# Start of a hybrid encoder block: input norm to first queries in a written order, norm weights as one row spread by TensorE, splits on VectorE, five PSUM banks for the first gates

## The chip, the cores and the metric

The kernel runs on one core of a Trainium2 chip. A core has TensorE (PE, matrix products; its weight loads are shown apart as PEld), VectorE (DVE), ScalarE (ACT) and GpSimd (POOL), which work side by side and wait for each other through semaphores; each takes its own instructions strictly in the order in which the program lists them. SyncE (SP) here only issues transfers. Operands lie in SBUF, the products of PE in PSUM banks of 128 x 512 fp32. The metric is the device time of one execution in microseconds, the median of three runs. A difference under about 0.2% can't be told from none.

## The reference

One layer of a bidirectional encoder over 1024 tokens of width 1024 with 16 learned meta tokens in front. All of it is fp32. The start, which is what this case is about, is

```python
a = rms_norm(h, norm_mix[l])                  # h: 16 meta rows, then x
(q_na, k_na, v_na, q_hg, z_f, z_b, i_hg, g_hg, gate_na, gate_hg) = split_cols(a @ w_in[l])
qh = silu(heads(q_hg))                        # 4 heads of 128
log_f = logaddexp(log(lb), log1p(-lb) + log_sigmoid(z))   # per direction
k = -expm1(log_f)
o = chunk_scan(qh, k_f, v, lf_f) + rev(chunk_scan(rev(qh), rev(k_b), rev(v), rev(lf_b)))
```

`rms_norm` multiplies each row by the inverse root of its mean square and by the weights `norm_mix`. Behind the recurrence (HGRN2) come a neighbourhood attention, two gated output projections, a product with `w_o`, an MLP with squared ReLU, and a last norm.

## The kernel before

**Products.** Every product with the input norm's result `a` is made of three: both operands are split into a high part (`hi`, rounded) and the rest (`lo`), and PE adds hi·hi, hi·lo and lo·hi in one PSUM bank (`mm3`, L134). `a` is kept transposed in `aT`: two halves of 512 tokens, each with a high and a low part of 8 x 128 rows; the 16 meta tokens are 16 more columns of half 0.

**The norm** (`norm_transpose`, L99) works on blocks of 128 rows: ACT squares the block with a running sum (`na`, L105), POOL makes the inverse root from it (`rtm`, `rs`, L92 and L93), DVE multiplies block, root and weights in one instruction (L107), PE transposes the result in two times four pieces (`pt`, L111), ACT rounds each four to the high part (L114), and DVE subtracts it to get the low part (L115). The weights `g_bc` are needed on all 128 partitions: one transfer reads the row 128 times (L155). The order is the meta block first, then blocks 0 to 7.

**The weight blocks.** `load_block` (L118) brings 1024 x 128 of `w_in` into `raw`, ACT makes `hi`, and another engine `lo`. There are two buffers of each. For the first two blocks, ZF and ZB (the forward and backward gates of head 0), `lo` is made by POOL, for all others by DVE.

**The gates of head 0** (`gates_of`, L250). ZF is three products: tokens 0 to 255, 256 to 511 with the 16 meta columns (272 columns), and 512 to 1023. ZB is two of 512. Two sigmoids on ACT (`sf`, `sn`) and three operations on DVE (into `T`, `X`, `Y`) evict each. The first three products are taken in the order ZF, ZF, ZB, then the second halves.

**Head 0's chain** (`hgrn`, L290). DVE multiplies neighbouring elements of `T` level by level (`TN`, L302). Queries: 48 products of block Q, two of 512 tokens; ACT a sigmoid, DVE `q` (L316) and `QQ` (L318). POOL adds X and Y to `kd` (L370); then PE makes the scores of `kd` and `q` (L374). For each level PE makes scores of `X` and `QQ` (L390), DVE makes the next `X` (a COPY of Y, L396, and a product, L397), and POOL the next `Y` (L399).

**The order of the work.** Each engine's list is set by the tile scheduler from the program text: an instruction may be placed earlier than it is written. Transfers are issued by SP in the order of the text. PSUM is eight banks: two `mm` and one `mx` for the products' turn, three `a` for transposes and scores, two `b`:

```python
psum_pools(mx=1, a=3, b=2)
```

Of the kernel before, what the change touches and what calls it, by code (L numbers as in the profile page):

```python
# [9 lines left out]
F32 = mybir.dt.float32  # L10
# [8 lines left out]
P = 128  # L19
# [29 lines left out]
def layer(ctx: ExitStack, tc: tile.TileContext, x, meta, w_in, w_na, w_hg, w_o, w_up, w_dn,  # L49
# [27 lines left out]
    psum_pools(mx=1, a=3, b=2)  # L77
# [21 lines left out]
    def norm_transpose(sp_pool, src, g_bc, dst, c0, n, nbuf):  # L99

        ssq = sp_pool.tile([P, 1], F32, tag="ssq", name="ssq", bufs=4)
        rs = sp_pool.tile([P, 1], F32, tag="rs", name="rs", bufs=4)
        tm = sp_pool.tile([P, 1], F32, tag="rtm", name="rtm", bufs=4)
        a = sp_pool.tile([P, D], F32, tag="na", name="na", bufs=nbuf)
        act.activation(a[:n], src, AF.Square, accum_out=ssq[:n])  # L105
        rsqrt_mean(rs[:n], ssq[:n], D, tm[:n])
        dve.scalar_tensor_tensor(a[:n], src, rs[:n], g_bc[:n], op0=ALU.mult, op1=ALU.mult)  # L107
        for j in range(2):
            pt = bank("a", "pt")
            for k in range(4):  # L110
                pe.transpose(pt[:, k, :n], a[:n, (4 * j + k) * P:(4 * j + k + 1) * P], ident[:n, :n])  # L111
            hi = dst[0][:, 4 * j:4 * j + 4, c0:c0 + n]
            lo = dst[1][:, 4 * j:4 * j + 4, c0:c0 + n]
            act.copy(hi, pt[:, :, :n])  # L114
            dve.tensor_tensor(lo, pt[:, :, :n], hi.bitcast(F32), op=ALU.subtract)  # L115


    def load_block(src, kc, scale=None, eng=dve):  # L118

        raw = wp.tile([P, KC, P], F32, tag="raw", name="raw")  # L120
        hi = wp.tile([P, KC, P], F32R, tag="hi", name="hi")
        lo = wp.tile([P, KC, P], F32R, tag="lo", name="lo")
        sp.dma_start(raw[:, :kc], src.rearrange("(k p) c -> p k c", p=P))
        if scale is None:
            act.copy(hi[:, :kc], raw[:, :kc])  # L125
            eng.tensor_tensor(lo[:, :kc], raw[:, :kc], hi[:, :kc].bitcast(F32), op=ALU.subtract)  # L126
# [19 lines left out]
    with tc.tile_pool(name="p0", bufs=1) as p0:  # L146
        g_bc = p0.tile([P, D], F32, name="g_bc")
        xm = p0.tile([NM, D], F32, name="xm")
        xt = [p0.tile([P, D], F32, tag="xt", name="xt", bufs=8) for _ in range(8)]

        def load_x(i):
            sp.dma_start(xt[i], x[i * P:(i + 1) * P, :])
        load_x(0)
        sp.dma_start(xm, meta)
        sp.dma_start(g_bc, g_mix.rearrange("(o d) -> o d", o=1).broadcast_to([P, D]))  # L155
        load_x(1)
        load_x(2)
# [1305 lines left out]
```

## Time and profile before

| | us |
|---|---|
| median of three runs | 1539.89 (1538.74 to 1540.42) |
| the profiled execution: its run, its span | 1543.13, 1541.4 |
| PE busy, of the span | 1500.9 (97%) |
| DVE, ACT, POOL busy | 1030.8, 658.0, 386.7 |
| mean granted clock of PE | 0.997 |

The profiled execution is one more run, 3.2 us above the median of the others. Its span is the time from the first to the last instruction on the core. A line of a timeline gives start, duration, engine, line of the kernel, operation, output and inputs, and in brackets how long the engine stood idle before it and what ended that.

### The profile page before, as it was taken

The numbers are of one execution on the slowest core, as the hardware profiler recorded it, in microseconds if no ns is written. First come the engines' busy times: TensorE is split into PE (matmuls) and PEld (weight loads), VectorE is DVE, ScalarE is ACT, GpSimd is POOL, SyncE is SP. The second block draws the span as 40 slices with busy tenths as digits, with TensorE's granted clock in tenths as the row PEclk, the third lists the DMA queues.
The fourth block names the chain that finished last, engine by engine and source line by source line (L and its number), as shares of the span: only waits on it lengthen the run. The fifth ranks groups of instructions, "written<-read, shape, count | busy, mean of one in ns | idle before, by whom it ended". The sixth has DMA issues, their size and how long they took to land.

```text
span 1541.4 us, 23453 instructions
## 1 busy us (share of the span) xinstructions
PE 1500.9 (97%) x9188; PEld 1253.1 (81%) x9188; DVE 1030.8 (67%) x1601; ACT 658.0 (43%) x1173; POOL 386.7 (25%) x355
## 2 busy tenths in 40 slices
PE   5999999999999999999999999999999999999998
PEld 5788888877888887888888887888888888888886
DVE  6666666664966877666566358877777544877876
ACT  6231313124665667434224135555555533434444
POOL 4313122216225310010000122444433200232142
PEclk9999999999999999999999999999999999999999
DMA  5101011113123127434747123444444676563224
GB/s 181 43 28 56 29 56 29 56 29 117 61 72 119 50 76 253 149 119 163 247 163 240 47 79 130 158 153 152 155 151 151 204 266 236 194 233 117 96 82 151
DMA packets 142591, 196.13 MB, mean 127 GB/s; under 512 B 8064, under 2 KB 90112, under 8 KB 142480
## 3 DMA queue, kind: packets, MB, share of 16 engines
q1 hardware_dynamic: 133680, 173.13, 34.0%
q10 hardware_dynamic: 6624, 14.16, 2.4%
q0 software_dynamic: 2176, 7.34, 1.3%
q8 instruction: 72, 1.18, 0.3%
q14 instruction: 39, 0.32, 0.1%
HBM read 140.08 MB, written 54.53 MB: 126 GB/s over the span
## 4 chain that ended last, share of the span: by engine, by line
PE 87%; DVE 6%; issue 2%; ACT 2%; DMA 1%; POOL 1%; SPq 0%; POOLq 0%; ACTq 0%; DVEq 0%
PE mm L135 11%; PE mm L136 10%; PE mm L137 10%; PE mm L1185 5%; PE pa L1185 4%; PE pb L692 4%; PE pb L694 4%; PE pb L693 4%; PE pb L1185 4%; PE pc L1185 4%; PE pc L692 3%; PE pc L694 3%; PE pc L693 3%; PE pa L694 2%; PE pa L692 2%
## 5 line engine op out<-in xcount | busy, mean ns | idle before, releaser
L135 PE MATMUL mm<-aT,hi 128*128 128x512 f32 (+2 forms) x640 | 229.8, 359 | 2.7 <-DVE QX L563 1.5
L137 PE MATMUL mm<-aT,lo 128*128 128x512 f32 (+2 forms) x640 | 227.5, 356 | 0.0
L136 PE MATMUL mm<-aT,hi 128*128 128x512 f32 (+2 forms) x640 | 226.3, 354 | 0.0
L135 PEld LDWEIGHTS mm<-aT,hi 128*128 128x128 f32 x640 | 121.6, 190 | 17.2 <-issue 1.7
L137 PEld LDWEIGHTS mm<-aT,lo 128*128 128x128 f32 x640 | 121.5, 190 | 13.1
L136 PEld LDWEIGHTS mm<-aT,hi 128*128 128x128 f32 x640 | 121.6, 190 | 12.5
L97 DVE TENSOR_TENSOR dl<-ur,dh 128x1024 fp32r<-128x1024 f32 x54 | 71.0, 1316 | 87.3 <-ACT dh L96 87.1
L96 ACT CAST dh<-ur 128x1024 fp32r<-128x1024 f32 x54 | 56.9, 1054 | 166.4 <-issue 91.1
L125 ACT CAST hi<-raw 128x1024 fp32r<-128x1024 f32 x36 | 37.8, 1051 | 106.6 <-PE mm L136 75.5
L990 DVE TENSOR_TENSOR wl<-raw,wh 128x512 fp32r<-128x512 f32 x50 | 41.0, 823 | 36.5 <-ACT wh L989 36.3
L994 ACT ACTIVATE uv<-uv 128x512 f32<-128x512 f32 x48 | 30.4, 633 | 80.0 <-DVE uv L1102 48.9
L990 DVE TENSOR_TENSOR wl<-sx,wh 128x512 fp32r<-128x512 f32 x70 | 61.0, 882 | 3.4 <-ACT wh L989 3.3
L989 ACT CAST wh<-sx 128x512 fp32r<-128x512 f32 x70 | 42.2, 620 | 42.2 <-PE pc L693 23.9
L1275 POOL TENSOR_TENSOR w<-w,tt 128x512 f32<-128x512 f32 x16 | 23.4, 1460 | 132.9 <-DVE tt L1274 113.6
L399 POOL TENSOR_TENSOR Y<-X,TN 128x512 f32<-128x512 f32 x20 | 34.9, 1746 | 86.1 <-DVE X L396 86.1
L126 DVE TENSOR_TENSOR lo<-raw,hi 128x1024 fp32r<-128x1024 f32 x34 | 43.2, 1269 | 16.1 <-ACT hi L125 15.3
L618 DVE CUSTOM_DVE_ANT_0 pr<-nsc,NB 128x432 f32<-128x432 f32 (+1 forms) x64 | 35.2, 559 | 26.6 <-PE nsc L613 26.5
L692 PE MATMUL pb<-nt,wh 128*128 128x512 f32 x128 | 50.2, 392 | 0.3 <-DVE uv L1072 0.2
L135 PE MATMUL mm<-wh,mT 128*128 128x512 f32 x128 | 50.2, 392 | 0.0
L92 POOL TENSOR_SCALAR rtm<-ssq 128x1 f32<-128x1 f32 (+1 forms) x17 | 6.5, 385 | 173.8 <-ACT junk L920 159.3
L693 PE MATMUL pb<-nt,wh 128*128 128x512 f32 x128 | 49.8, 389 | 0.0
L694 PE MATMUL pb<-nt,wl 128*128 128x512 f32 x128 | 49.8, 389 | 0.0
(388 smaller groups left out, 4406.1 us busy)
## 6 DMA issues: line engine op xcount, KB each, us to landing
raw<-in_w_in SPq DMA_DIRECT2D x56, 512.0 KB, 4.0
ur<-usp SPq DMA_DIRECT2D x54, 512.0 KB, 3.4
raw<-in_w_up SPq DMA_DIRECT2D x16, 1024.0 KB, 6.1
usp<-us SPq DMA_DIRECT2D x60, 256.0 KB, 2.2
sg<-gsp SPq DMA_DIRECT2D x16, 512.0 KB, 3.7
w<-in_w_dn SPq DMA_DIRECT2D x16, 512.0 KB, 4.9
usp<-uv SPq DMA_DIRECT2D x30, 256.0 KB, 2.2
gsp<-gv ACTq DMA_DIRECT2D x24, 256.0 KB, 2.6
```

Source lines behind the costliest of these rows:

```text
L96: act.copy(hi, src)
L97: dve.tensor_tensor(lo, src, hi.bitcast(F32), op=ALU.subtract)
L126: eng.tensor_tensor(lo[:, :kc], raw[:, :kc], hi[:, :kc].bitcast(F32), op=ALU.subtract)
L135: pe.matmul(ps, lh, rh, start=first, stop=False)
L136: pe.matmul(ps, lh, rl, start=False, stop=False)
L137: pe.matmul(ps, ll, rh, start=False, stop=last)
L692: pe.matmul(ps, lhs[0][:, c], rhs[0][:, k], start=first and k == 0, stop=False, skip_group_check=True)
L693: pe.matmul(ps, lhs[0][:, c], rhs[1][:, k], start=False, stop=False, skip_group_check=True)
L694: pe.matmul(ps, lhs[1][:, c], rhs[0][:, k], start=False, stop=k == 3, skip_group_check=True)
L989: act.copy(v(hi), src)
L990: dve.tensor_tensor(v(lo), src, v(hi).bitcast(F32), op=ALU.subtract)
L1185: pe.matmul(ps, a[n == 2][:, q, j * P:(j + 1) * P], b[n == 1][:, q], start=first and n == 0, stop=last and n == 2, skip_group_check=True)
```

## The change

**Norm weights.** A transfer of one row of 1024 numbers, issued by ACT, takes the place of the transfer of 128 rows. PE multiplies a column of ones with the row in two products of 512 columns (`pg`), and ACT copies them to `g_bc`, ahead of its first square. The meta rows, the gates' bounds `lt` and the gain are issued by ACT as well.

**Splits.** `load_block` has no engine any more: `lo` is made by DVE for all blocks.

**Banks.** The start uses two `mm`, three `mx` and three `a`; the two `b` come in place of two `mx` once head 0's queries are written. So the five first gate products each have a bank of their own, and none of them needs an eviction to begin.

**Order.** Everything from the first instruction to head 0's queries stands inside `tc.manual_schedule`, where each engine's list is the order of the text. The text has a new function `start`, which lists the steps block by block: square, transpose, scale, evict, and some of the gate products between them. The gates' evictions are called after all five products.

```diff
-    psum_pools(mx=1, a=3, b=2)
+    psum_pools(mx=3, a=3)
...
-    def load_block(src, kc, scale=None, eng=dve):
+    def load_block(src, kc, scale=None, raw=None):
...
-            eng.tensor_tensor(lo[:, :kc], raw[:, :kc], hi[:, :kc].bitcast(F32), op=ALU.subtract)
+            dve.tensor_tensor(lo[:, :kc], raw[:, :kc], hi[:, :kc].bitcast(F32), op=ALU.subtract)
...
-        sp.dma_start(g_bc, g_mix.rearrange("(o d) -> o d", o=1).broadcast_to([P, D]))
...
+        act.dma_start(g_row, g_mix.rearrange("(o d) -> o d", o=1))
+        act.dma_start(xm, meta)
+        act.dma_start(lt.rearrange("p a b c -> p (a b c)"), lbl)
+        act.dma_start(gain_sb, gain)
...
+        for h in range(2):
+            pg = bank("a", "pg").rearrange("p a b -> p (a b)")
+            pe.matmul(pg, ones, g_row[:, h * TH:(h + 1) * TH], start=True, stop=True)
+            act.copy(g_bc[:, h * TH:(h + 1) * TH], pg)
...
+        square(0)
+        scale(0)
+        square(1)
+        pt = transpose(0)
+        scale(1)
+        evict(0, pt)
+        blocks[0] = load_block(None, KC, raw=raw_f)
+        square(2)
+        pt = transpose(1)
+        scale(2)
+        evict(1, pt)
+        square(3)
...
+        f0 = products(0, 0, 0, 256, 0, 0)
+        some(f0, 4)
+        square(4)
+        pt = transpose(3)
+        scale(4)
+        evict(3, pt)
+        some(f0, 4)
+        square(5)
+        pt = transpose(4)
+        blocks[1] = load_block(None, KC, raw=raw_b)
+        scale(5)
+        evict(4, pt)
+        b0 = products(1, 0, 0, TH, 0, 0)
+        some(b0, 2)
+        square(8)
+        pt = transpose(5)
+        scale(8)
+        square(6)
+        scale(6)
+        evict(5, pt)
+        some(b0, 3)
+        ptm = transpose(8)
+        evict(8, ptm)
+        pt = transpose(6)
+        square(7)
+        scale(7)
+        evict(6, pt)
+        some(b0, 3)
+        pt = transpose(7)
...
+        evict(7, pt)
...
+        for q in (products(0, 0, 256, 256, 256, NM), products(0, 1, 0, TH, TH, 0), products(1, 1, 0, TH, TH, 0)):
+            some(q, KC)
...
+        early[C_Q] = block_of(C_Q)
...
+    with tc.manual_schedule(engines={e.engine for e in (pe, act, dve, pool, sp)}):
+        start()
...
         list(ahead[0])
...
+        cur = hgrn(0, hp, lmask_get, tiles[0], ahead[1])
+        next(cur)
+    psum_pools(mx=1, a=3, b=2)
```

`some(f0, 4)` is four steps of three products each; block 8 is the meta block. Three places of the lists follow. In them L105 and L507 are squares, L114 and L528 the casts of a transposed block, L125 and L112 the `hi` of a weight block.

ACT's list in the norm, before and then of the change:

```order
L105 ACTIVATE na,ssq<-xm 16x1024
L105 ACTIVATE na,ssq<-xt 128x1024 x2
L114 CAST aT_90<-pt 128x4x16 x2
L105 ACTIVATE na,ssq<-xt 128x1024
L114 CAST aT_90<-pt 128x4x128
L125 CAST hi<-raw 128x1024
L114 CAST aT_90<-pt 128x4x128 x2
L105 ACTIVATE na,ssq<-xt 128x1024
L114 CAST aT_90<-pt 128x4x128 x3
L105 ACTIVATE na,ssq<-xt 128x1024 x2
L114 CAST aT_90<-pt 128x4x128 x2
```

```order
L498 COPY g_bc<-pg 128x512 x2
L507 ACTIVATE na,ssq<-xt 128x1024 x2
L528 CAST aT_87<-pt 128x4x128 x2
L112 CAST hi<-raw 128x1024
L507 ACTIVATE na,ssq<-xt 128x1024
L528 CAST aT_87<-pt 128x4x128 x2
L507 ACTIVATE na,ssq<-xt 128x1024
L528 CAST aT_87<-pt 128x4x128 x2
L507 ACTIVATE na,ssq<-xt 128x1024
L528 CAST aT_87<-pt 128x4x128 x2
L507 ACTIVATE na,ssq<-xt 128x1024
L112 CAST hi<-raw 128x1024
```

Now the copies of the weights stand first, and squares and pairs of casts alternate.

PE's list of the change at its beginning (L497 spreads the weights, L520 transposes, L122 to L124 are the three products of a step):

```order
L497 MATMUL pg<-g_row,ones 128x512 x2
L520 MATMUL pt<-ident,na 128x128 x24
L122 MATMUL mm<-aT_87,hi 128x256
L123 MATMUL mm<-aT_88,hi 128x256
L124 MATMUL mm<-aT_87,lo 128x256
```

The transposes of three blocks stand ahead of the first product; before it was those of the meta block and of two blocks.

DVE's list from the products of `T` to the second `q`, before and then of the change (L261 is `TN`, L355 and L356 the next `X`, L275 `q`, L277 `QQ`, L113 the `lo` of a weight block):

```order
L302 TENSOR_TENSOR TN<-TN 128x256
L396 COPY X<-Y 128x128x4
L302 TENSOR_TENSOR TN<-TN 128x128
L316 TENSOR_TENSOR q<-q,mm 128x512
L302 TENSOR_TENSOR TN<-TN 128x64
L318 TENSOR_TENSOR QQ<-T_385,q 128x2x512
L302 TENSOR_TENSOR TN<-TN 128x32
L397 TENSOR_TENSOR X<-X,TN 128x128x2x2
L302 TENSOR_TENSOR TN<-TN 128x16
L396 COPY X<-Y 128x64x8
L397 TENSOR_TENSOR X<-X,TN 128x64x2x4
L126 TENSOR_TENSOR lo<-raw,hi 128x1024
```

```order
L355 COPY X<-Y 128x128x4
L261 TENSOR_TENSOR TN<-TN 128x128
L356 TENSOR_TENSOR X<-X,TN 128x128x2x2
L261 TENSOR_TENSOR TN<-TN 128x64
L355 COPY X<-Y 128x64x8
L261 TENSOR_TENSOR TN<-TN 128x32
L356 TENSOR_TENSOR X<-X,TN 128x64x2x4
L261 TENSOR_TENSOR TN<-TN 128x16
L113 TENSOR_TENSOR lo<-raw,hi 128x1024
L275 TENSOR_TENSOR q<-q,mm 128x512
L277 TENSOR_TENSOR QQ<-T_524,q 128x2x512
L113 TENSOR_TENSOR lo<-raw,hi 128x1024
```

`q` stood behind one COPY of `Y`, now behind two, behind all the `TN` and behind a `lo`.

More of the change, by code (lines that the diff above doesn't have):

```diff
@@ L278, in gate @@
             return ev, (mev if d == 0 else None)
+        if done:
+            for d, ps, t0, n, nm in done:
+                ev, mev = gate(d)
+                if nm:
+                    mev(ps[:, n:])
+                ev(ps[:, :n], t0, n)
+            return
         zf = proj_steps(C_ZF + hd * P, *gate(0))
         zb = proj_steps(C_ZB + hd * P, *gate(1))
-        if hd == 0:
-            for z in (zf, zf, zb):
-                yield next(z)
         for z in (zf, zb):
```

151 lines of the change are left out of this document (94 added, 57 removed).

## The prediction

> **What bounds the kernel now.** I read the page first, then the busy time in stretches (a row has its start and end, its length, the busy time of PE, PEld, DVE, ACT and POOL, and PE's granted clock), then the instructions of the first 80 us.
>
> ```profile
> PE 1500.9 (97%) x9188; PEld 1253.1 (81%) x9188; DVE 1030.8 (67%) x1601; ACT 658.0 (43%) x1173; POOL 386.7 (25%) x355
> ...
> 9.00:32.10 23.10, 16.42 (x106) 15.25 (x106) 20.53 (x21) 16.15 (x30) 13.64 (x16) 1.00 0.54 194
> 32.10:61.10 29.00, 29.00 (x135) 23.87 (x135) 16.85 (x37) 10.95 (x22) 11.67 (x17) 1.00 0.20 58
> 61.10:70.00 8.90, 6.28 (x156) 5.74 (x156) 7.66 (x13) 1.73 (x3) 3.63 (x2) 0.85 0.21 61
> ```
>
> TensorE (PE) is busy 97% of the span; of its 40.5 us of idle time 18.3 lie before 70 us (the first 9.0, and the two pieces below). So whatever moves the first score products of head 0 moves the end by the same amount. The change acts in the two places where PE is short of work: the norm, where it stands idle for 6.7 of the 23.1 us from 9 to 32.1, and 61.1 to 70, where 2.62 are missing. In between it has no gap.
>
> The norm, in the timelines of DVE, ScalarE (ACT), GpSimd (POOL) and PE:
>
> ```profile
> 9.04 1.27 DVE L107 SCALAR_TENSOR_TENSOR na<-xm,rs,g_bc 16x1024 f32<-16x1024 f32 x1 [9.04 <-DMA g_bc<-in_g_mix]
> 10.24 1.27 DVE L107 SCALAR_TENSOR_TENSOR na<-xt,rs,g_bc 128x1024 f32<-128x1024 f32 x1
> ...
> 12.28 1.28 DVE L107 SCALAR_TENSOR_TENSOR na<-xt,rs,g_bc 128x1024 f32<-128x1024 f32 x1 [0.38 <-POOL rs L93]
> 14.28 3.48 DVE L107 SCALAR_TENSOR_TENSOR na<-xt,rs,g_bc 128x1024 f32<-128x1024 f32 x1 [0.71 <-ACT hi L125]
> ...
> 24.07 1.28 DVE L107 SCALAR_TENSOR_TENSOR na<-xt,rs,g_bc 128x1024 f32<-128x1024 f32 x1 [1.27 <-POOL rs L93]
> ...
> 26.47 1.27 DVE L107 SCALAR_TENSOR_TENSOR na<-xt,rs,g_bc 128x1024 f32<-128x1024 f32 x1
> ...
> 28.87 3.08 DVE L107 SCALAR_TENSOR_TENSOR na<-xt,rs,g_bc 128x1024 f32<-128x1024 f32 x1
> ...
> 35.88 1.29 DVE L115 TENSOR_TENSOR aT<-pt,aT 128x512 fp32r<-128x512 f32 x2 [0.27 <-ACT aT L114]
> ...
> 4.62 1.05 ACT L105 ACTIVATE na<-xm 16x1024 f32<-16x1024 f32 x1 [2.62 <-DMA xm<-in_meta]
> ...
> 10.18 1.06 ACT L105 ACTIVATE na<-xt 128x1024 f32<-128x1024 f32 x1 [3.37 <-DMA xt<-in_x]
> ...
> 26.35 1.08 ACT L114 CAST aT<-pt 128x512 fp32r<-128x512 f32 x2
> 27.31 1.07 ACT L125 CAST hi<-raw 128x1024 fp32r<-128x1024 f32 x1
> ...
> 14.33 2.35 POOL L126 TENSOR_TENSOR lo<-raw,hi 128x1024 fp32r<-128x1024 f32 x1
> ...
> 24.25 1.16 POOL L92 TENSOR_SCALAR rtm<-ssq 128x1 f32<-128x1 f32 x1 [0.21 <-ACT na L105]
> 26.43 0.19 POOL L92 TENSOR_SCALAR rtm<-ssq 128x1 f32<-128x1 f32 x1 [0.39 <-ACT na L105]
> ...
> 11.56 1.97 PE L111 MATMUL pt<-ident,na 128*128 128x128 f32 x8 [0.17 <-DVE na L107]
> ...
> 25.71 1.03 PE L111 MATMUL pt<-ident,na 128*128 128x128 f32 x8
> ```
>
> DVE starts at 9.04, when the 512 KB broadcast of the weights has landed, and its last eviction ends at 37.17. A block costs it 2.40 (24.07 to 26.47). Twice a scaling lasts 3.48 or 3.08 instead of 1.28; the first stands exactly beside POOL's split of 2.35.
>
> **The change part by part.** The sum is made against the profiled execution (span 1541.4, run 1543.13); the median of the runs is 3.2 us below that, and I carry the difference over to 1539.89.
>
> *Weights as one row.* The broadcast goes. The row leaves ACT's queue first; the 64 KB transfer of xm, the nearest row, is there at 4.62, and 4.0 is my estimate for 4 KB. The two products of 128x512 on PE are not in the trace: by the transposes, eight of 128 columns in 1.97 at the cold start, 512 columns are about 1.0 each; twice that if a plain fp32 product takes two passes. I take 1.35, two are 2.7, to 6.7. Two copies follow, 0.54 each (half of the 1.08 pair), the second behind its product: 7.3. Block 0's square stands behind them on ACT. From a square's start to its scaling takes 2.1 (10.18 to 12.28), so block 0 is scaled at 9.4 instead of 10.24: a gain of 0.8, between 0 and 1.7. Four small transfers are now issued by ACT, which has nothing else to do until the first product ends, and SP's queue loses four issues: block 1's x, whose square waited for it until 10.18, comes earlier and is hidden. Meta's block, which was scaled first, moves behind block 5 with the same work.
>
> *Splits from POOL to DVE.* DVE takes two more operations, 1.14 each (the period from 64.82 to 65.95, quoted below), and gets back 2.2 and 1.8 of the two stretched scalings: a net gain of 1.7. POOL's small operations are no longer queued behind 2.35. The Trainium skill ("SBUF — State Buffer", Who interferes with whom) says that a DVE operation with two SBUF inputs and a POOL operation that reads SBUF exclude each other for a whole instruction. The trace agrees (14.28 lasts until POOL's split is done). The rule also speaks against the change: the splits on DVE have two such inputs, and POOL's small operations will wait behind them, as the 1.16 against 0.19 shows; by it each of the 2.1 us steps below that meets a split or a scaling takes 1.0 more, and the norm's +2.6 becomes +3.6 to +4.6; by the unstretched rows it stays.
>
> *The written order of the norm.* DVE's busy time in the norm was 37.17 - 9.04 less its idle time, 28.1 - 2.8 (0.38, 0.71, 1.27, 0.27 and 0.16 of an unquoted wait) = 25.3; now 25.3 - 4.0 + 2.3 = 23.6. Without gaps it would end at 9.4 + 23.6 = 33.0. But each square now stands on ACT behind the casts of the block two before it, where before it ran up to two blocks ahead. The loop of two blocks is scaling 1.2, eight transposes 1.03 (1.97 at the slow clock), casts 1.08, square to scaling 2.1: 5.4 warm and 6.35 slow, against 4.8 of DVE's own work. Step by step: block 0 scaled at 9.4; block 2 behind a slow loop and the split's 1.05 on ACT, 16.8; block 4 one slow loop later, 23.2. Block 3's transposes stand behind 12 products of 256 columns on PE, which ran at half clock (0.21 from start to start) in the first 3 us:
>
> ```profile
> 22.11 0.41 PE L137 MATMUL mm<-aT,lo 128*128 128x256 f32 x1
> 22.32 0.41 PE L135 MATMUL mm<-aT,hi 128*128 128x256 f32 x1
> ...
> 29.35 0.29 PE L136 MATMUL mm<-aT,hi 128*128 128x272 f32 x1
> 29.47 0.29 PE L137 MATMUL mm<-aT,lo 128*128 128x272 f32 x1
> ...
> 49.83 0.39 PE L137 MATMUL mm<-aT,lo 128*128 128x512 f32 x1
> 50.06 0.39 PE L135 MATMUL mm<-aT,hi 128*128 128x512 f32 x1
> ```
>
> Twelve take 2.5. Block 2's transposes end at 16.8 + 3.2 = 20.0, block 3's at about 24.0, its casts at 25.1, and block 5's square follows. The second block's hi ends at 27.3, its lo holds DVE to 28.5, and block 5 is scaled then. The casts of block 4 end at 28.4; the squares of meta and block 6 behind them give scalings at 30.5 and 31.7. PE meanwhile: 6 products (1.4), block 5's transposes to 31.0, 9 products (2.05) to 33.1, meta's transposes to 34.1, its casts (0.5), block 7's square, and block 7 is scaled at 36.7. Its transposes end at 38.8. Behind them stand 24 products of 272 columns at 0.125 and 48 of 512 at 0.23: 3.0 + 10.9. Head 0's last gate product ends at 52.7 instead of 50.06: **+2.6**. Bounds: DVE without a gap brings the last transposes to 31.2 (33.0 less 1.8: the last two evictions, 1.29, and half a pair of casts) and the product to 45.1, -5.0; slow transposes throughout and POOL's small operations stretched each time add some 3: +5.5. I take the value of the steps, since every one is a row.
>
> *Five banks.* With them the 272 and 512 products need no eviction before they start. Evictions were no bound before (PE is busy for all of the 29 us from 32.1 to 61.1), so this removes nothing.
>
> *Gates to first queries.* On ACT the split of Q's block now stands ahead of all sigmoids, and it waits for the buffer that the last ZF product frees, 5.5 before ZB's end. Priced as casts (1.08 a pair) the six sigmoids of the first half, four of the second and the split take some 5 to 6, so they just fit under ZB's last product and I cost them at nothing; without that cover it would be up to 1.
>
> On DVE q stands behind the second COPY X<-Y and behind the split of the next block, not in front of them.
>
> ```profile
> 53.24 1.22 DVE L302 TENSOR_TENSOR TN<-T 128x1024 f32<-128x1024 f32 x1
> ...
> 56.36 0.43 DVE L302 TENSOR_TENSOR TN<-TN 128x256 f32<-128x256 f32 x1
> 59.92 0.43 DVE L396 COPY X<-Y 128x512 f32<-128x512 f32 x1 [3.13 <-POOL Y L399]
> ...
> 60.47 0.68 DVE L316 TENSOR_TENSOR q<-q,mm 128x512 f32<-128x512 f32 x1
> ...
> 64.82 1.21 DVE L126 TENSOR_TENSOR lo<-raw,hi 128x1024 fp32r<-128x1024 f32 x1
> 65.95 0.67 DVE L316 TENSOR_TENSOR q<-q,mm 128x512 f32<-128x512 f32 x1
> ...
> 53.41 4.53 POOL L370 TENSOR_TENSOR kd<-X,Y 128x512 f32<-128x512 f32 x1 [10.69 <-DVE X L270]
> 58.02 1.87 POOL L399 TENSOR_TENSOR Y<-X,T 128x512 f32<-128x512 f32 x1
> 60.43 1.52 POOL L399 TENSOR_TENSOR Y<-X,TN 128x512 f32<-128x512 f32 x1 [0.54 <-DVE X L396]
> 64.37 2.79 POOL L399 TENSOR_TENSOR Y<-X,TN 128x512 f32<-128x512 f32 x1 [2.42 <-DVE X L396]
> ...
> 61.29 0.46 PE L374 MATMUL sc<-q,kd 128*32 128x32 f32 x32 [0.19 <-DVE q L316]
> 66.77 0.46 PE L374 MATMUL sc<-q,kd 128*32 128x32 f32 x32 [2.43 <-DVE q L316]
> 68.72 1.08 PE L390 MATMUL sc<-QQ,X 128*32 128x32 f32 x64
> ```
>
> Let z be the end of the last gate product. The chain of TN began at 53.24, z + 3.2; the 1.14 of the split in front of it are gone, so it begins at z + 2.1. To the end of the TN of 256 it takes 3.5: z + 5.6. POOL's second kd ended 1.2 after that chain (57.94 against 56.79): z + 6.8. Y 1.87: z + 8.7. COPY and the next Y, 0.5 + 1.52 (2.79 if DVE works beside it): z + 10.7 to 12.0. Then COPY and TN 0.45 (0.55 in front of q before, with a wider TN), X 0.6 (priced as q, whose width it has), TN 0.1, the split 1.14, q 0.6: z + 13.6 to 14.9. I take 14.2, and 0.2 until PE starts: the first scores at z + 14.4. Q's 48 products end at z + 10.9, and behind the scores on PE stands everything else: a stall of 3.5, where it was 0.19. The second stall of 2.43 goes: what stood between the first and the second q before (TN, X, COPY, X) now stands ahead of both, only QQ (1.13) and one split (1.14) are left, so the second q is done 2.9 after the first, and PE has 3.05 of work there (61.29 to 64.34). Together 3.5 against 2.62: **+0.9**, between 0.4 and 1.6. The first level's scores (68.72 = z + 18.7) so come at z + 19.5.
>
> Sum: 2.6 + 0.9 = +3.5, and 1539.9 + 3.5 = **1543.4**. About 3.1 us (0.2%) is what can be told from no change, so this is just beyond it.
>
> **The rivals.**
>
> A, *the norm without gaps*: ACT's squares are early enough and DVE sets the pace. For it: DVE had only 2.8 of idle time between 9.04 and 37.17. Against: the written order forbids squares ahead. z at 45.1, then + 0.9: -4.1, 1535.8. It decides from z at 46 on, where -4.0 + 0.9 passes 0.2%. A half way, with the gaps as they were (2.8), gives z at 47.9, -2.1 + 0.9 = -1.2: 1538.7, no change (B).
>
> C, *the slow clock lingers*: PE at half clock loses as much as the window holds. Around the stall of 2.43 the clock from 61.1 to 70 is 0.85, so 1.3 of the 8.9 us are lost. A stall of over 3.5, or the waits between the first transposes and products, can hold a second and third window: 1.7 each by my estimate, somewhat more than that one; +3.5 + 3.4 = +6.9, 1546.8; with the upper bound of the norm 1549. The Trainium skill ("TensorE: Matmul & The Clock Gate", What's actually happening) halves the clock after an idle window of 3.4 us. The trace departs from it, since a stall of 2.43 was enough; by the rule only the new stall would be long enough, which would add the 1.7 of one window to the sum, and by the trace both are.
>
> D, *the change doesn't bind*: if POOL finishes the second kd early, no q is late; then the stall is under 2.6 and only the norm's +2.6 is left, 1542.5, no change.
>
> **How the numbers follow.** Forecast (1541.5 to 1545.5) 0.36, A 0.18, B and D 0.28, C 0.18. Of the forecast's share about 0.06 lies within 0.2%. Faster 0.18, same 0.34, slower 0.48. The range 1535.5 to 1549.5 runs from A to C's end; the forecast's own is 1541.5 to 1545.5.
>
> **What will show it.** The scaling of block 0 near 9.4 (A, B and the forecast share it). The period between scalings: 2.4 under A, 2.7 to 3.2 under the forecast, with idle time before them that ACT or POOL ends. The last gate product at 52.7 (45 under A, 48 under B). An idle time of 3.5 before the first scores, ended by q, and none before the second; under D it is under 2.6. The clock after it: more than one stretch of ten below 0.9 is C. I am wrong if the last gate product ends before 50, or if the stall falls on another instruction than q.

## The result, and the profile after

The change made the kernel slower: 1547.7 us in the median (1545.37 to 1551.14, 4 runs) against 1539.71, a ratio of 1.0054 with a 95% interval of 1.0034 to 1.0074. Timed once more with the experiments it was 1547.44 (6 runs) against 1541.1 of before, 1.0035 (1.0023 to 1.0047). Forecast was 1543.4: the direction is right, the size was 6 to 8 us by the medians (5.4 and 8.3 by the ratios) and not 3.5.

The single profiled executions stand closer together than the medians: 1541.4 and 1543.6 of span. The first was 3.2 above the median of before, the second was the fastest of its four; a second profile of the changed kernel (r_after) has 1545.4. So the readings below go by a mark inside the trace, the start of the third level's scores: 75.24 before, 79.89 and 81.79 after (+4.7 and +6.6). In the timelines of PE, before and after:

```profile
75.24 0.38 PE L390 MATMUL sc<-QQ,X 128*32 128x32 f32 x18
```

```profile
79.89 0.38 PE L349 MATMUL sc<-QQ,X 128*32 128x32 f32 x18
```

Behind the mark the shift does not stay the same. By the rows of ACT the changed kernel is 4.4 us (first profile) and 6.4 us (second) behind up to about 469 us, 2.7 and 4.6 at 555 us, and 2.2 and 4.0 at the end. From 470 to 560 us its PE waits 0.8 to 0.9 us for DVE, where before it waits 2.2. Another part differs from one execution to the next: near 590 us PE runs at half clock for 3.4 us in the profiles of before and r_after and not in the first profile of the change, although that is the kernel of r_after. So these three executions can't say how much of the loss at the mark reaches the end; the medians say about all of it.

The profile of e5_bcast fell on a disturbed execution and is not used; the same kernel was profiled again as e5b_bcast.

PE in stretches, after (start and end, length, busy us of PE, PEld, DVE, ACT, POOL, then PE's granted clock):

```profile
9.00:32.10 23.10, 17.22 (x98) 14.46 (x99) 19.62 (x24) 15.27 (x29) 6.20 (x14) 0.93 0.48 171
32.10:61.10 29.00, 28.69 (x145) 23.90 (x143) 13.59 (x32) 11.29 (x24) 13.62 (x17) 1.00 0.08 22
61.10:70.00 8.90, 2.40 (x40) 2.19 (x40) 8.87 (x13) 1.53 (x2) 3.24 (x2) 0.70 0.18 54
```

Up to 61.1 PE is as busy as before: 17.22 and 28.69 against 16.42 and 29.00. The loss is in the third row: 2.40 of 8.9 us busy, where it was 6.28, and a clock of 0.70 where it was 0.85. The timelines of that stretch, PE, DVE and POOL:

```profile
67.77 0.66 PE L333 MATMUL sc<-q,kd 128*32 128x32 f32 x32 [6.50 <-DVE q L275]
...
52.38 1.22 DVE L261 TENSOR_TENSOR TN<-T 128x1024 f32<-128x1024 f32 x1
...
61.01 0.43 DVE L355 COPY X<-Y 128x512 f32<-128x512 f32 x1 [5.09 <-POOL Y L358]
...
65.82 1.21 DVE L113 TENSOR_TENSOR lo<-raw,hi 128x1024 fp32r<-128x1024 f32 x1
66.95 0.67 DVE L275 TENSOR_TENSOR q<-q,mm 128x512 f32<-128x512 f32 x1
...
48.72 0.52 POOL L394 TENSOR_TENSOR tm<-fm 128x8 f32<-128x8 f32 x1 [10.30 <-DVE fm L231]
...
51.49 5.05 POOL L390 TENSOR_TENSOR km<-km,tm 128x8 f32<-128x8 f32 x3
56.50 2.53 POOL L329 TENSOR_TENSOR kd<-X,Y 128x512 f32<-128x512 f32 x2
59.11 1.87 POOL L358 TENSOR_TENSOR Y<-X,T 128x512 f32<-128x512 f32 x1
```

PE waits 6.50 us for the first q. q stands on DVE behind a COPY that waits 5.09 for POOL's Y. And Y is late because POOL was busy from 48.72 to 56.50 with seven operations on at most eight columns (`tm`, `km`), which belong to the meta keys of a much later step; only then came the two `kd`. Before, the seven ran at 39.3 to 41.5, in 2.2 us, and held nobody up; the last three of them, in POOL's timeline of before:

```profile
40.62 0.87 POOL L431 TENSOR_TENSOR km<-km,tm 128x8 f32<-128x8 f32 x3
```

The second stall before the scores (2.43 before) is gone, as forecast.

The norm, DVE and PE and ACT:

```profile
8.65 1.28 DVE L512 SCALAR_TENSOR_TENSOR na<-xt,rs,g_bc 128x1024 f32<-128x1024 f32 x1 [8.65 <-POOL rs L93]
10.66 1.29 DVE L512 SCALAR_TENSOR_TENSOR na<-xt,rs,g_bc 128x1024 f32<-128x1024 f32 x1 [0.72 <-POOL rs L93]
...
15.52 1.28 DVE L512 SCALAR_TENSOR_TENSOR na<-xt,rs,g_bc 128x1024 f32<-128x1024 f32 x1 [0.73 <-POOL rs L93]
...
21.50 1.28 DVE L512 SCALAR_TENSOR_TENSOR na<-xt,rs,g_bc 128x1024 f32<-128x1024 f32 x1 [1.11 <-POOL rs L93]
...
33.86 1.28 DVE L512 SCALAR_TENSOR_TENSOR na<-xt,rs,g_bc 128x1024 f32<-128x1024 f32 x1 [1.74 <-POOL rs L93]
...
2.27 3.74 PE L497 MATMUL pg<-g_row,ones 1*128 1x512 f32 x4 [2.27 <-DMA g_row<-in_g_mix]
...
11.15 0.59 ACT L528 CAST aT<-pt 128x512 fp32r<-128x512 f32 x1 [2.42 <-PE pt L520]
```

The row is there at 2.27, its products take 3.74, block 0 is scaled at 8.65. DVE waits for the root in front of blocks 1, 2, 4 and 7 (0.72, 0.73, 1.11 and 1.74). Still the last gate product ends at 50.24 (51.73 in the second profile), hardly later than the 50.06 of before.

### The profile page after: what moved, and what is told of

Read it like the earlier page. It is cut to its first block, busy times and chain, and to the rows that moved or that the text cites. A ratio compares the mean times of both kernels' runs of the same rounds, so it can differ in the third digit from the quotient of the medians.

```text
span 1543.6 us, 23460 instructions
## 1 busy us (share of the span) xinstructions
PE 1503.5 (97%) x9192; PEld 1252.5 (81%) x9192; DVE 1029.1 (67%) x1603; ACT 658.8 (43%) x1175; POOL 379.9 (25%) x354
## 4 chain that ended last, share of the span: by engine, by line
PE 88%; DVE 5%; issue 3%; ACT 2%; POOL 2%; DMA 1%; POOLq 0%; ACTq 0%; DVEq 0%
PE mm L122 11%; PE mm L123 10%; PE mm L124 10%; PE mm L1297 5%; PE pa L1297 4%; PE pb L804 4%; PE pb L806 4%; PE pb L805 4%; PE pc L1297 4%; PE pb L1297 4%; PE pc L806 3%; PE pc L804 3%; PE pc L805 3%; PE pa L806 2%; PE pa L804 2%
## 5 line engine op out<-in xcount | busy, mean ns | idle before, releaser
L122 PE MATMUL mm<-aT,hi 128*128 128x512 f32 (+2 forms) x640 | 230.2, 360 | 2.5 <-DVE QX L675 1.5
L124 PE MATMUL mm<-aT,lo 128*128 128x512 f32 (+2 forms) x640 | 227.3, 355 | 0.5 <-DVE lo L113 0.5
L122 PEld LDWEIGHTS mm<-aT,hi 128*128 128x128 f32 x640 | 121.8, 190 | 16.8 <-issue 1.7
L124 PEld LDWEIGHTS mm<-aT,lo 128*128 128x128 f32 x640 | 121.7, 190 | 14.1 <-DVE lo L113 1.0
L112 ACT CAST hi<-raw 128x1024 fp32r<-128x1024 f32 x36 | 37.8, 1050 | 105.8 <-PE mm L123 75.1
L1102 DVE TENSOR_TENSOR wl<-sx,wh 128x512 fp32r<-128x512 f32 x70 | 61.1, 883 | 3.4 <-ACT wh L1101 3.3
L113 DVE TENSOR_TENSOR lo<-raw,hi 128x1024 fp32r<-128x1024 f32 x36 | 45.1, 1252 | 16.0 <-ACT hi L112 15.9
L122 PE MATMUL mm<-wh,mT 128*128 128x512 f32 x128 | 50.1, 392 | 0.0
L124 PE MATMUL mm<-wh,mT 128*128 128x512 f32 x128 | 49.8, 389 | 0.0
```

The source lines that it names most:

```text
L113: dve.tensor_tensor(lo[:, :kc], raw[:, :kc], hi[:, :kc].bitcast(F32), op=ALU.subtract)
L122: pe.matmul(ps, lh, rh, start=first, stop=False)
L124: pe.matmul(ps, ll, rh, start=False, stop=last)
L1102: dve.tensor_tensor(v(lo), src, v(hi).bitcast(F32), op=ALU.subtract)
```

## The experiments

All runs in one table. z is the end of head 0's last gate product, taken as the start of Q's first one; the stalls are PE's idle time before the first and the second half of the first scores, "third" is the start of the third level's scores (all us, of one profile). Ratios are to before, in the same series (its median there was 1541.0 to 1541.8, and 1539.7 beside the change's first).

| run | z | stalls | third | median | ratio (95%) |
|---|---|---|---|---|---|
| before | 50.06 | 0.19, 2.43 | 75.24 | 1541.1 | 1 |
| the change, first | 50.24 | 6.50, 0 | 79.89 | 1547.7 | 1.0054 (1.0034 to 1.0074) |
| r_after | 51.73 | 6.49, 0 | 81.79 | 1547.44 | 1.0035 (1.0023 to 1.0047) |
| e1_km | 50.97 | 4.04, 0 | 78.04 | 1544.70 | 1.0021 (1.0013 to 1.0030) |
| e2_q | 50.26 | 0, 5.12 | 78.64 | 1545.06 | 1.0025 (1.0016 to 1.0034) |
| e3_gates | 50.84 | 3.86, 0 | 77.75 | 1544.31 | 1.0020 (1.0011 to 1.0029) |
| e4_q2_gates | 50.37 | 0.09, 0 | 74.81 | 1540.32 | 0.9999 (0.9991 to 1.0007) |
| e5_bcast | no profile used | | | 1543.96 | 1.0020 (1.0010 to 1.0029) |
| e5b_bcast | 50.39 | 6.54, 0 | 80.61 | 1544.20 | 1.0020 (1.0011 to 1.0029) |
| e6_poolsplit | 55.96 | 6.50, 0 | 85.45 | 1552.36 | 1.0074 (1.0062 to 1.0086) |
| e7_squares | 48.92 | 6.49, 0 | 78.25 | 1544.37 | 1.0026 (1.0016 to 1.0036) |
| e9_squares | 48.14 | 0.04, 2.21 | 73.02 | 1539.66 | 0.9992 (0.9983 to 1.0001) |
| e10_bcast | 49.21 | 0.03, 2.21 | 74.10 | 1540.03 | 0.9994 (0.9985 to 1.0003) |
| e11_lo_late | 47.80 | 0.03, 1.19 | 70.82 | 1539.03 | 0.9983 (0.9974 to 0.9992) |

The median less the third level's start is 1465.5 to 1467.8 in all rows but two (e5b_bcast 1463.6, e11_lo_late 1468.2), while the third level's start runs from 70.8 to 85.5. So what the start costs, the kernel costs, to within about 2 us. That the five first gate products each have a bank of their own was not tested by itself.

### The changed kernel again

> The changed kernel once more, for a second profile and a closer time. Theory 1 (the loss is made before 75 us, by one stall in front of the first scores): last gate product at 50.1 +- 0.3, stall before the first scores 6.5 +- 0.3, first-level scores near 73.7, and the rest of the kernel shifted by 4 to 5 us to the end; the times then lie 4 to 6 us above before. Rival (something later loses too): the second profile shows a further shift of 2 us or more behind 80 us, and the median stays 8 us above before.

The stall is 6.49, the third level comes 6.6 later than before, the time is 6.3 above before. Theory 1 holds for the stall and for the place of the loss: behind 82 us the shift against before is never larger than at that mark, where the rival wanted 2 us more. z and the time lie outside the ranges of theory 1. z came 1.5 later than in the first profile: the row landed at 2.97 and not at 2.27, and the clock rose later, since the gate products of 256 columns start 0.21 apart until 22 us and not only until 20.2 (0.12 apart behind that).

### GpSimd's small operations behind the second Y

```diff
-                pool.tensor_tensor(fap(Y, h, mid3), fap(X, h, mid3),
+                yi = pool.tensor_tensor(fap(Y, h, mid3), fap(X, h, mid3),
...
+                if lv == 1:
+                    kdi = yi
...
+        after_kd = ExitStack()
+        if hd == 0:
+            after_kd.enter_context(tc.issue_after(kdi.ins))
...
+        after_kd.close()
```

> GpSimd's seven small operations on the meta keys (km, tm) stand behind the second Y, everything else as changed. Theory 1a (these operations, starved by DVE's burst of gate evictions, hold up both kd and so Y and q): kd ends at about 57.1 instead of 59.0, the first Y at 59.0 instead of 61.0, and the stall before the first scores shrinks from 6.5 to 4.5, about -2 us. Theory 1b (POOL is held by DVE's chain of TN in any case): kd still ends at 59, the stall stays 6.5, the time stays.

The timelines of PE and POOL:

```profile
66.04 0.51 PE L333 MATMUL sc<-q,kd 128*32 128x32 f32 x32 [4.04 <-DVE q L275]
...
51.27 2.06 POOL L329 TENSOR_TENSOR kd<-X,Y 128x512 f32<-128x512 f32 x1 [12.12 <-DMA raw<-in_w_in]
54.22 2.20 POOL L329 TENSOR_TENSOR kd<-X,Y 128x512 f32<-128x512 f32 x1 [0.89 <-DVE X L225]
56.85 2.19 POOL L358 TENSOR_TENSOR Y<-X,T 128x512 f32<-128x512 f32 x1 [0.43 <-DVE X L355]
```

kd ends at 56.42 and Y starts at 56.85 instead of 59.11, though z is 0.7 later. The stall is 4.04: theory 1a. The small operations cost 2.5 us, and it is their place in POOL's list that does it. The rest of the stall has another cause now: DVE does not wait at all from 48.4 us to the first q (POOL's first Y is done before the COPY that needs it), but some of its operations last longer beside POOL, such as a product X of 2.83 us at 57.23, beside Y, where it took 1.13 in the changed kernel.

### q ahead of the second COPY

```diff
-            dve.tensor_tensor(QQ[:, :, t0:t0 + TH], T0[:, :, t0:t0 + TH], q2, op=ALU.mult)
+            qi.append(dve.tensor_tensor(QQ[:, :, t0:t0 + TH], T0[:, :, t0:t0 + TH], q2, op=ALU.mult))
...
-                dve.tensor_copy(fap(Xn, h, mid), fap(Y, h, mid))
...
+                with tc.issue_after(qi[0].ins) if hd == 0 and lv in (1, 2) else ExitStack():
+                    dve.tensor_copy(fap(Xn, h, mid), fap(Y, h, mid))
```

> DVE's second and third COPY X<-Y, with their products, stand behind the first QQ, so q no longer waits for GpSimd's Y; everything else as changed. Theory 2 (q's place makes the stall): no stall over 0.5 before the first scores, which start at 61.2 to 61.6; first-level scores at 67 to 68 instead of 73.7; 5 to 6 us less than the changed kernel, about 1541. Theory 1a alone (GpSimd's lateness bounds the scores through kd): the stall stays above 4.

The timelines of PE and DVE:

```profile
69.38 0.66 PE L334 MATMUL sc<-q,kd 128*32 128x32 f32 x32 [5.12 <-DVE q L276]
...
55.55 3.60 DVE L261 TENSOR_TENSOR TN<-TN 128x256 f32<-128x256 f32 x5
...
60.20 0.68 DVE L276 TENSOR_TENSOR q<-q,mm 128x512 f32<-128x512 f32 x1
60.91 2.18 DVE L278 TENSOR_TENSOR QQ<-T,q 128x1024 f32<-128x1024 f32 x1
...
65.41 0.43 DVE L357 COPY X<-Y 128x512 f32<-128x512 f32 x1 [1.38 <-POOL Y L360]
...
66.35 2.29 DVE L113 TENSOR_TENSOR lo<-raw,hi 128x1024 fp32r<-128x1024 f32 x1
68.56 0.67 DVE L276 TENSOR_TENSOR q<-q,mm 128x512 f32<-128x512 f32 x1
```

And that of POOL:

```profile
56.57 2.54 POOL L330 TENSOR_TENSOR kd<-X,Y 128x512 f32<-128x512 f32 x2
```

The first scores start at 61.23 without a stall, so q's place did make the first stall. But the whole chain that stood in front of the first q now stands in front of the second, and PE waits 5.12 there. Of the 5 to 6 us expected, 2.4 came. Neither theory is enough alone: POOL's Y is late, and a q that stands behind it waits, by 1.38 directly and by a QQ and a `lo` that last about 1 us longer beside POOL's Y (2.18 and 2.29).

The row at 55.55 shows how the two engines hurt each other: five `TN` take 3.60 here, while POOL does its kd, and 1.42 in e4_q2_gates, where kd is done by then:

```profile
58.17 1.42 DVE L261 TENSOR_TENSOR TN<-TN 128x256 f32<-128x256 f32 x5
```

The Trainium skill ("SBUF — State Buffer", Who interferes with whom) says that a DVE instruction with two SBUF inputs contends with a GpSimd instruction that reads SBUF, and that the ports they share are an exclusive lock; the trace agrees.

### First gates evicted before Q's block is split

```diff
-        for q in (products(0, 0, 256, 256, 256, NM), products(0, 1, 0, TH, TH, 0), products(1, 1, 0, TH, TH, 0)):
-            some(q, KC)
-        firsts.sort(key=lambda q: (q[2] >= TH, q[0], q[2]))
-        early[C_Q] = block_of(C_Q)
+        some(products(0, 0, 256, 256, 256, NM), KC)
...
+        def done():
+            yield from sorted(firsts, key=lambda q: (q[0], q[2]))
+            some(products(0, 1, 0, TH, TH, 0), KC)
+            some(products(1, 1, 0, TH, TH, 0), KC)
+            early[C_Q] = block_of(C_Q)
+            yield from firsts[3:]
```

> The first three gate products are evicted before the weight block of Q is split, as before the change; the order of q stays as changed. Theory 1a: km and the first kd are done by 45, the second kd ends at 57, Y at 59, the stall before the first scores is 4.0 to 4.5, about -2 us. Theory 2 expects the same here, since q still stands behind Y. If the stall goes below 1, the burst alone was the cause and q's place costs nothing.

The timelines of PE and POOL:

```profile
65.74 0.49 PE L333 MATMUL sc<-q,kd 128*32 128x32 f32 x32 [3.86 <-DVE q L275]
...
41.52 0.85 POOL L390 TENSOR_TENSOR km<-km,tm 128x8 f32<-128x8 f32 x3
42.65 1.29 POOL L329 TENSOR_TENSOR kd<-X,Y 128x512 f32<-128x512 f32 x1 [0.29 <-DVE X L225]
52.87 2.19 POOL L329 TENSOR_TENSOR kd<-X,Y 128x512 f32<-128x512 f32 x1 [8.93 <-DVE X L225]
```

The last three km take 0.85 and not 5.05 when DVE is not in the middle of its burst. The stall is 3.86, about what e1_km gave by another way. It does not go below 1, so q's place costs as well. The cause of the larger part of the 3.0 us by which the stall exceeded its forecast of 3.5 is settled: the evictions were put into one run behind the split of Q's block, and POOL's list could not move past them.

### Both orders mended

Edit: that of e3_gates, and of e2_q with the second QQ:

```diff
+                with tc.issue_after(qi[1].ins) if hd == 0 and lv in (1, 2) else ExitStack():
```

> Both in one: the first three gate products evicted before Q's block is split, and the second and third COPY X<-Y with their products behind the second QQ, so neither q waits for GpSimd's Y. Theory (the stall is the two orders together, GpSimd's small operations behind a burst and q behind Y): no stall over 0.5 before either half of the first scores, first-level scores at 66.5 to 67.5 (before 68.72, changed 73.6 to 75.5); 6 to 8 us less than the changed kernel, 1 to 3 us less than before, about 1539. Rival: the Y chain, now late, stalls a later level by as much; then the third level's scores stay above 77 and the time above 1543.

No stall is left before the first scores, and the loss is gone: 1540.32, the same as before within 0.1%. But the rival was partly right. PE and DVE:

```profile
70.44 0.77 PE L350 MATMUL sc<-QQ,X 128*32 128x32 f32 x64 [1.74 <-DVE QQ L374]
...
66.19 1.91 DVE L358 TENSOR_TENSOR X<-X,TN 128x512 f32<-128x512 f32 x1
68.02 1.10 DVE L374 TENSOR_TENSOR QQ<-QQ,T 128x512 f32<-128x512 f32 x1
```

The X that was put off now stands in front of the next QQ, and the second level waits 1.74 for it. The third level comes at 74.81, only 0.4 earlier than before, though 2.5 us of stalls ahead of it are gone. It is not the loss above 1543 that the rival expected.

### Weights by broadcast again

> The norm weights come by the 512 KB broadcast on SP's queue behind block 0 again, without the two products and copies; everything else as changed. Theory (the row brings forward the whole norm): block 0 is scaled at 9.5 to 10.5 instead of 8.65, and the last gate product comes 1.0 to 1.5 later, as does everything behind. Rival (the norm's pace is set further on by ACT and PE, not by its start): the last gate product stays within 0.5 of the changed kernel's 50.2 to 51.7.

> The kernel of e5_bcast once more, since its profile was of a disturbed execution; its time there was 1543.96, some 3 us under the changed kernel's 1547.4. New theory (the row is the slower way here: two cold products, two copies and block 0's square stand in line behind it, while the broadcast, second on SP's queue, lands by 6.6): block 0 is scaled at 6.9 again, the last gate product comes 1 to 2.5 earlier than with the row (50.2 to 51.7), the stall before the first scores stays 6.5, and the time is 2 to 4 us less than the changed kernel. Old theory (the row brings the norm forward): the last gate product comes later than 51.5.

The edit, behind block 0's transfer on SP's queue:

```diff
-        act.dma_start(g_row, g_mix.rearrange("(o d) -> o d", o=1))
+        sp.dma_start(g_bc, g_mix.rearrange("(o d) -> o d", o=1).broadcast_to([P, D]))
...
-            pe.matmul(pg, ones, g_row[:, h * TH:(h + 1) * TH], start=True, stop=True)
-            act.copy(g_bc[:, h * TH:(h + 1) * TH], pg)
```

DVE's timeline in e5b_bcast:

```profile
6.97 1.28 DVE L504 SCALAR_TENSOR_TENSOR na<-xt,rs,g_bc 128x1024 f32<-128x1024 f32 x1 [6.97 <-POOL rs L93]
10.63 1.28 DVE L504 SCALAR_TENSOR_TENSOR na<-xt,rs,g_bc 128x1024 f32<-128x1024 f32 x1 [2.37 <-POOL rs L93]
```

The first theory fell: second on the queue, the broadcast is faster than the row, and block 0 is scaled at 6.97 against 8.65. Block 1 gains nothing (10.63 against 10.66), and z is 50.39, within what two profiles of the changed kernel span; so the new theory is right for block 0 alone. The medians of both series are 3.2 to 3.5 us under that of r_after, but the ratios to before, 1.0020 twice against 1.0035, have intervals that meet: a gain is likely and not certain. The profiles show no place for it, and it stays open. In e10_bcast, below, the same edit gave nothing.

### Splits on GpSimd again

```diff
-            dve.tensor_tensor(lo[:, :kc], raw[:, :kc], hi[:, :kc].bitcast(F32), op=ALU.subtract)
+            eng.tensor_tensor(lo[:, :kc], raw[:, :kc], hi[:, :kc].bitcast(F32), op=ALU.subtract)
...
+        blocks[0] = load_block(None, KC, raw=raw_f, eng=pool)
...
+        blocks[1] = load_block(None, KC, raw=raw_b, eng=pool)
```

> The low parts of the first two weight blocks are made by GpSimd again; everything else as changed. Theory (DVE and GpSimd exclude each other, as the scaling of 3.48 beside the split of 2.35 showed before): a scaling beside each split lasts 3.0 to 3.5, the small operations behind it come later, and the last gate product comes 0.5 to 2 later. Rival (in the written order DVE has gaps that take in the splits): no difference over 0.5 in the last gate product.

The timelines of DVE, POOL and PE:

```profile
16.96 1.28 DVE L512 SCALAR_TENSOR_TENSOR na<-xt,rs,g_bc 128x1024 f32<-128x1024 f32 x1 [3.59 <-POOL rs L93]
...
26.26 3.43 POOL L113 TENSOR_TENSOR lo<-raw,hi 128x1024 fp32r<-128x1024 f32 x1
...
18.39 1.94 PE L520 MATMUL pt<-ident,na 128*128 128x128 f32 x8 [4.36 <-DVE na L512]
...
29.74 0.79 PE L124 MATMUL mm<-aT,lo 128*128 128x512 f32 x1 [2.77 <-POOL lo L113]
```

z is 4 to 6 later and the time 4.9 us more, so in this order the place of the splits is worth more than either theory had. The way is another than expected: no scaling is stretched, but the roots queue behind the split on POOL (3.59), and PE waits for the split itself (2.77).

### Squares ahead of the casts

The squares of blocks 2 to 5, of block 7 and of the meta block move ahead of casts that they stood behind; of one of them:

```diff
+        square(4)
...
-        square(4)
```

> Each square stands on ACT ahead of the casts of the block two before it, no longer behind them; everything else as changed. Theory (the written order holds the norm): DVE's waits for the inverse root (0.7, 0.7, 1.1, 1.7) go or halve, and the last gate product comes 2 to 3 earlier, at about 48. Rival (PE's own work, cold transposes and products, sets the pace behind 17 us): it stays at 50 to 51. In both the stall before the first scores stays at 6.5.

DVE's waits for the root in front of blocks 2, 4 and 7 are gone, z comes at 48.92, 1.3 to 2.8 earlier, and the median is 3.1 us less (by the ratios, 1.0026 against 1.0035, that is not clear of noise). The stall stays 6.49. Two waits of 1.4 and 1.5 for casts came in their place (before 22.46 and 35.42 in DVE's timeline), which is probably why z does not come the full 3 earlier.

### A version from the parts

> The first gates evicted early, the squares ahead of the casts, and of the late COPYs the second stands behind the first QQ and the third behind the second QQ. Theory (the parts add): last gate product at about 49, no stall over 0.5 before the first scores, and the second level is no longer stalled by 1.7 as with both COPYs behind the second QQ; third level's scores at 71.5 to 73.5 (before 75.24, both COPYs late 74.81), time about 1538, 2 to 4 us under before. Rival (the chain of X, Y and QQ on DVE and GpSimd bounds the levels whatever the order): third level's scores at 74 or later, and no gain on before.

The early gates of e3_gates, the squares of e7_squares, and the second COPY behind the first QQ, the third behind the second (the edit is against e4_q2_gates):

```diff
-                with tc.issue_after(qi[1].ins) if hd == 0 and lv in (1, 2) else ExitStack():
+                with tc.issue_after(qi[lv - 1].ins) if hd == 0 and lv in (1, 2) else ExitStack():
```

z is 48.14, and the third level comes at 73.02, as the theory had it. The time, 1539.66, can't be told from before (0.9983 to 1.0001). The stall only moved to the second half of the scores, in the timelines of DVE and PE:

```profile
61.18 2.54 DVE L113 TENSOR_TENSOR lo<-raw,hi 128x1024 fp32r<-128x1024 f32 x1
63.64 0.68 DVE L276 TENSOR_TENSOR q<-q,mm 128x512 f32<-128x512 f32 x1
...
64.47 0.46 PE L334 MATMUL sc<-q,kd 128*32 128x32 f32 x32 [2.21 <-DVE q L276]
```

> As e9_squares, with the norm weights by the broadcast, second on SP's queue, instead of the row. Theory: block 0 is scaled near 6.9, the last gate product comes another 1 to 2 earlier, at 47 to 48, and the time is 1 to 2 us under e9_squares, about 1536.5. Rival (block 1's x, landing at 8.6, and the cold transposes set the pace): no difference to e9_squares over 0.5.

The edit is that of e5_bcast on e9_squares. The time shows no difference to e9_squares: the rival. Block 0 is scaled earlier (7.31 against 8.94), block 1 is not (10.92 against 10.95), and z and the third level come 1.1 later in this profile.

On e9_squares, the splits that stand between two score steps are issued behind the second QQ:

```diff
-                between()
+            with ExitStack() as late:
+                if hd == 0 and lv == 0:
+                    late.enter_context(tc.issue_after(qi[1].ins))
+                    late.enter_context(tc.issue_after(si[1].ins))
+                between()
```

> As e9_squares, and the split of head 1's forward gate block (hi on ACT, lo on DVE) stands behind the second q and QQ, not between the two q. Theory (the 2.2 us stall before the second half of the first scores is this split, 2.54 long beside GpSimd's Y): the stall falls below 0.5, the third level's scores come at 71 to 72.5 instead of 73.0, and the time is 1 us less than e9_squares, about 1538.5. Rival (DVE has no slack from 50 to 75 us, so the split only moves the wait on): a stall of 1 or more before the first or second level's scores, third level's scores within 0.7 of 73.0, no gain.

The timelines of DVE and PE:

```profile
60.84 0.68 DVE L276 TENSOR_TENSOR q<-q,mm 128x512 f32<-128x512 f32 x1
...
61.67 0.46 PE L334 MATMUL sc<-q,kd 128*32 128x32 f32 x32 [1.19 <-DVE q L276]
```

Without the split in front of it the second q ends 2.8 earlier than in e9_squares (61.52 against 64.32). The stall shrinks by less, from 2.21 to 1.19, because PE has only 8 products between the two halves of the scores and not 20; waits of 0.49 and 0.68 follow before the first and the second level. So the stall that the rival expected is there, and the gain is there too: the third level comes at 70.82. 1539.03 against 1541.75 is 0.9983 (0.9974 to 0.9992), faster than before by an amount at the edge of what can be told. The gain in the median, 2.7, is less than the 4.4 us at that mark. The spans of the two profiled executions, 1541.4 and 1537.0, do differ by 4.4: that of before lay above its median in this series by 1.4, that of e11_lo_late below by 0.3.

## Why the prediction was right, and where its size was wrong

The direction is right, and so is the reason for it in the forecast: q stands behind POOL's Y, and PE waits for q. The size is not: the norm lost less than forecast (0.2 to 1.7 against 2.6), and the stalls grew by 3.9 and not by 0.9. The measured time lies within the stated range only because the range reached up to C's end, and C's mechanism was not what happened. That is luck. The prediction's signs of being wrong did not come: z is not before 50, and the stall stands on q.

**The stall before the first scores, +0.9 forecast.** This term failed, in its step from the chain of TN to the first q. It was built on "POOL's second kd ended 1.2 after that chain", a distance taken from before, where POOL's list was empty in front of kd. In the changed list the seven small operations stand there. I had counted what the change moves on DVE and ACT, and not asked what on POOL hangs on the gates that now come late. The chain of TN does begin at z + 2.1 as forecast (52.38), so ACT's split did fit under the last gate product; but kd ends at 59.03, z + 8.8 and not z + 6.8. Behind that, DVE's X and its last TN took 2.01 and 1.23 beside POOL's Y instead of 0.6 and 0.1, and q ends at z + 17.4 and not z + 14.2. With the small operations out of the way (e1_km, e3_gates) the stall is 4.04 and 3.86; with them it is 6.5. That 4.04 and 3.86 are close to the 3.5 of the working is in part luck: there kd ends earlier than in the working (z + 5.4 and z + 4.2), and DVE's chain to the TN of 256, beside it, later (z + 9.4 and z + 8.2, not z + 5.6). From z to the third level it is 29.7 and 30.1 instead of 25.2: +4.5 to +4.9.

**The clock, rival C.** Two pieces of half clock came instead of one, as C had it, but they cost little more. PE of before, in its second stall and at half clock, and then PE of the change, in its stall, at half clock and from there to the third level:

```profile
61.30:66.70 5.40, 3.04 (x52) 2.79 (x52) 5.37 (x10) 1.16 (x2) 2.98 (x2) 1.00 0.00 0
66.70:70.70 4.00, 3.93 (x107) 3.60 (x108) 2.80 (x3) 0.37 (x1) 0.46 (x1) 0.57 0.47 135
```

```profile
61.30:67.70 6.40, 0.00 (x0) 0.00 (x0) 6.37 (x11) 1.33 (x2) 3.24 (x2) 0.76 0.00 0
67.70:71.50 3.80, 3.73 (x46) 3.69 (x47) 3.77 (x4) 0.00 (x0) 0.00 (x0) 0.50 0.52 153
71.50:79.90 8.40, 7.86 (x204) 6.73 (x202) 5.56 (x11) 0.68 (x3) 0.00 (x0) 1.00 0.21 60
```

Before lost (1 - 0.57) x 4.0 = 1.7 to the clock. After, most of the first piece lies inside the stall (6.4 us at 0.76), where PE has nothing to do, and what is lost is half of 3.8: 1.9. In r_after it is half of 4.8, 2.4. So the clock adds 0.2 to 0.7, and C's 3.4 is refuted. The 4.5 to 4.9 from z to the third level are the stalls, 6.50 instead of 2.62 (+3.9), the clock, and a wait at the second level of 0.54 instead of 0.20.

**The norm, +2.6 forecast.** Measured z is 50.24 and 51.73: +0.2 and +1.7. Block 0's time was near (9.4 against 8.65 and 9.35), and the cause of DVE's longer waits was right: they are for the root, and e7_squares takes away the three that stand behind casts (blocks 2, 4 and 7). Too long was the loop: "eight transposes, casts" were added in line, while the first cast starts after four transposes (11.15, with PE's transposes from 9.99 on), and so runs beside the other four. Block 2 is scaled at 15.52 and not 16.8, block 4 at 21.50 and not 23.2, block 7 at 33.86 and not 36.7. Within block 0's time two errors cancelled: PE's products of the row, 1.87 each, were dearer than the 1.35 taken, and the row came sooner, at 2.27 and not at 4.0.

**The splits, a net gain of 1.7 for DVE.** Right in sign. Undone in the new order they cost 4.9, by waits for POOL; no scaling is stretched there, so the 1.7 itself, a count of stretched scalings, is not shown.

**The second stall, 2.43 that goes.** Right: 0 in every run in which q kept its place.

**What moves the end.** The sum took every us before the first scores as one at the end. By the medians that holds within about 2 us over all runs; in the single profiles 2.2 and 4.0 of the 4.7 and 6.6 were left at the end.

**Rivals.** A (a norm without gaps, z at 45) and B (z at 47.9) are refuted by z and the waits, D by the stall. The measured 6.3 and 8.0 are of the size of C's 6.9, but not by its mechanism: the norm costs less than forecast (0.2 to 1.7), the clock little (0.2 to 0.7), and the stalls 3.9 instead of 0.9.

## What to carry to other kernels

When a change moves a whole group of work later, walk down the list of every engine, not only of those that the group runs on, and ask what waited for its first pieces: here seven tiny operations for a later step were pulled in front of the ones that matter. Moving an instruction past another need not remove a wait: in e2_q, e4_q2_gates and e9_squares a part of it came back at the next reader (5.12, 1.74 and 2.21 us). The whole loss went only where work also left the crowded stretch: the gates' evictions to an earlier time (e4_q2_gates), then the split to a later one (e11_lo_late). And compare two kernels by a mark inside the traces as well as by the spans, when single executions differ by as much as the effect.

## What the runs showed of the hardware

An operation on 128 x 8 numbers took POOL 1.7 us in the mean when DVE worked without a pause beside it (three `km` 5.05 in the changed kernel, against 0.85 in e3_gates, where DVE had pauses). Small work on POOL is not cheap in a burst of DVE.

Half clock on PE comes in pieces of about 3.4 us, and idle times far under that are enough for one. In e4_q2_gates, PE in the 3.4 us before the drop and in the 3.4 behind it:

```profile
67.90:71.30 3.40, 1.66 (x72) 1.40 (x71) 3.40 (x7) 0.00 (x0) 0.25 (x1) 1.00 0.00 0
71.30:74.70 3.40, 3.40 (x13) 2.71 (x13) 3.40 (x7) 0.32 (x2) 2.10 (x2) 0.50 0.00 0
```

PE was idle for 1.74 of the first 3.4 us, half of it, and had been at work again for 0.8 us when the clock fell. 2.21 us in e9_squares, 2.43 of before, 3.86 in e3_gates and 4.04 in e1_km gave one piece too, 5.12 in e2_q and 6.5 in the changed kernel two, and 1.19 in e11_lo_late none. The Trainium skill ("TensorE: Matmul & The Clock Gate", What's actually happening) gives a window of about 3.4 us that runs freely, and an idle window as the condition. The length agrees, and so does the free run: in the changed kernel the clock fell at 16.9 and at 64.7 us, 47.8 apart, which is fourteen times 3.41. The condition, if read as a window without any work, doesn't agree. That about half a window of idle time is enough would fit all of these, but was not tried by itself.

The granted clock of a window is of use only behind the first change of clock that a trace records. In the first row of the result it reads 0.93 for the changed kernel and 1.00 for before, yet the products of both start 0.21 apart at first and 0.12 apart later, and r_after shows 1.00 up to 67 us with the same products. Early in a kernel the distance of equal products is the better clock.
